# Decays between the tokens of a chunk: differences of running sums in place of masked products summed by TensorE

## The chip, the cores and the metric

The kernel runs on one core of one Trainium2 chip. The metric is the device time of one execution in microseconds, taken as the median of several executions. TensorE is called PE in the profile (PEld its weight loads), VectorE DVE, ScalarE ACT, GpSimd POOL, and SP is the queue that issues the transfers.

## The reference, cut to what matters

The reference is a two-layer backbone for 256 context tokens and 256 latent tokens of width 1,024. Each layer mixes the tokens with three parallel head groups (an S5 scan, a gated delta rule with 4 heads, a Mamba-2 block with 16 heads), each in both directions, and then applies a feed-forward block (dense in layer 0, eight experts in layer 1). What the change touches are the decays between tokens of one chunk. With `cs` the running sum of a head's log decays along the chunk, the reference forms

```python
def seg_decay(cs):
    """cs (..., T) cumulative log-decays -> (..., T, T) with [i, j] = exp(cs_i - cs_j) for i >= j, else 0."""
    diff = cs[..., :, None] - cs[..., None, :]
    return jnp.where(mask, jnp.exp(jnp.where(mask, diff, 0.0)), 0.0)
```

and multiplies it into the products of queries and keys. All log decays are negative or zero, so a decay is at most 1. The second direction reads the tokens backwards.

## The kernel before, in words

Everything is laid out for 512 tokens (context and latent together) as four token tiles of 128. The method `mixer` builds one layer's token mixing: it normalises the tokens into `hH` and `hL`, projects them with `proj` (weights are streamed by `wload`, which copies each into a rounded half `wH` on ACT, line 321, and a remainder `wL` on DVE, line 322, and `mm3` multiplies the three products of halves), convolves (`conv_silu`, four multiply-adds `cv_acc` on DVE at line 800), runs the S5 scan (`s5B`, `s5t`, lines 609 and 612 on DVE), the delta rule (`gdn_prep`, `gdn` with its triangular inverses `iv_X`, `iv_Q`) and Mamba-2 (`m2`).

The order of the instructions on every engine is fixed when the program is built. A planner places instructions by the priority of the band in which they are written (`self.band(...)`, numbers out of the table `Q`; a lower number is more urgent) and by its own estimate of when their inputs are there. Each engine then works through its list in order, and an instruction at the head that still waits holds up all behind it.

`smalls` computes, for each token, the 40 log decays `la` (two directions of 16 Mamba-2 heads and 4 delta-rule heads). It splits them into a rounded half and a remainder, `la2` (lines 742 to 746), and sums them along the tokens with six small matmuls per layer (lines 755 to 761).

`decay_quad` (lines 769 to 781) makes the decays of 4 heads and one token tile, both directions multiplied together: a tile of 128 by 4 times 128. For each direction GpSimd writes a tile `dq_r` (line 776): 8 columns of `la2` (4 heads, both halves), each spread over 128 columns and masked by an affine select. TensorE multiplies it twice (halves) by a triangular matrix `tri_r`, all four products into one bank of PSUM, and ACT takes the exponential out of the bank (line 781). There are 32 such calls: in each layer 4 in `gdn_prep` (line 856, one per token tile, result `gd_W`, banks `px`, one buffer for `dq_r`), and in `m2_decays` (lines 1060 to 1067, result `dq_W`, written to the scratch `WD` by a transfer, banks `bg`, two buffers for `dq_r`) 16 in layer 0 and 8 in layer 1, where only the two latent tiles need them. This is 64 affine selects and 128 matmuls in all. The banks `bg` are three in layer 0 (5, 6, 7) and two in layer 1 (6, 7); `px` has two (2, 3) while `gdn_prep` runs. `m2` loads the decays back from `WD` (line 1158), some time later.

Of the kernel before, what the change touches and what calls it, by code (L numbers as in the profile page):

```python
# [10 lines left out]
F32 = mybir.dt.float32  # L11
F32R = mybir.dt.float32r
# [38 lines left out]
NC16 = 50  # L51


def _cst():
# [7 lines left out]
    out += [c16 == r % 16, c16 > r % 16, c16 < r % 16, (r // 16) % 2 == np.arange(2)[None, :]]  # L62
    return np.concatenate([np.asarray(m, np.float32) for m in out], axis=1)
# [27 lines left out]
class Net:  # L91
    def __init__(self, ctx, tc, A, out, dump=None):
# [10 lines left out]
        cst = c.tile([128, ncst * 128 + NC16], F32, name="cst")  # L103
# [17 lines left out]
        self.tri_r = c.tile([128, 2, 128], F32R, name="tri_r")  # L121
        nc.vector.tensor_copy(self.tri_r[:, 0, :], self.gt)
        nc.vector.tensor_copy(self.tri_r[:, 1, :], self.lt)
# [585 lines left out]
    def smalls(self, l, p, tp, h):  # L709
# [44 lines left out]
        lav = la.rearrange("p t (d h) -> p d t h", d=2)  # L754
        for d in range(2):
# [11 lines left out]
        return dict(sp=sp, dde=dde, la=la2.bitcast(F32), beta=beta, cs=ex[:, 0], de=ex[:, 1], tot=ex[:, 2])  # L767

    def decay_quad(self, p, sm, t, h0, out, tag, bufs):

        nc = self.nc
        ps = self.ps(tag)
        for d in range(2):
            r = p.tile([128, 8, 128], F32R, name="dq_r", bufs=bufs)
            v = sm["la"][:, t, d * 5 + h0 // 4].rearrange("p x h -> p (x h)")
            nc.gpsimd.affine_select(r, v.unsqueeze(2).to_broadcast([128, 8, 128]), pattern=[[0, 8], [1 if d == 0 else -1, 128]],
                                    compare_op=OP.is_ge, fill=0.0, base=0, channel_multiplier=-1 if d == 0 else 1)
            for x in range(2):
                self.mm(ps, self.tri_r[:, d, :], r[:, x * 4:x * 4 + 4].rearrange("p h c -> p (h c)"), start=(d + x == 0),
                        stop=(d + x == 2))  # L780
        nc.scalar.activation(out, ps.rearrange("p (h c) -> p h c", h=4), AF.Exp)
# [1214 lines left out]
```

## Time and profile before

| quantity | value |
|---|---|
| time, median of 3 executions | 2483.29 us (2481.88 to 2485.01) |
| time of the profiled execution | 2479.87 us |
| span of the profiled execution | 2478.1 us |
| busy share of the span: PE, DVE, ACT, POOL | 93%, 75%, 57%, 10% |
| mean granted clock of TensorE | 0.974 of full |

The span is the stretch between the first and the last instruction of one profiled execution; its time is 1.8 us longer, and the median of the timed executions is 3.4 us above that. The shares are means over stages that are limited by different engines, so a stage has to be read by itself. Layer 0's mixer lies at about 60 to 600 us, layer 1's at about 1,120 to 1,600 us, and the experts fill the rest.

### The profile page before, as it was taken

Reading aid. Unit: us, or ns where it says so; the run is one execution under the profiler, and the core shown is the slowest. Engines: PE = TensorE matmul, PEld = TensorE weight load, DVE = VectorE, ACT = ScalarE, POOL = GpSimd, SP = SyncE. Lnnn points to the kernel's source line nnn. Section 1 sums busy time; section 2 is a strip of 40 time slices with the busy share of each in tenths; the row PEclk is TensorE's granted clock in tenths of the full one; section 3 lists DMA queues with packets and bytes.
Section 4 is the critical chain, followed back from the end, with each engine's and each line's share of the span. In section 5 each row is a group of like instructions: output and inputs, shape, how many; then the busy total and the mean of one; then the engine's idle time right before and its main releaser. Section 6 shows DMA issues by size and latency. Waiting matters only on the chain.

```text
span 2478.1 us, 36217 instructions
## 1 busy us (share of the span) xinstructions
PE 2296.1 (93%) x12886; PEld 1843.6 (74%) x12886; DVE 1868.1 (75%) x3138; ACT 1419.7 (57%) x2200; POOL 257.3 (10%) x332
## 2 busy tenths in 40 slices
PE   7999887898999999998998799889999999999998
PEld 4878675666767777886887677778887888888876
DVE  8887995576577773436679867678888888888887
ACT  4765475343335343235764844357777777677765
POOL 0011553212000000000021522100000000000000
PEclk9999998997999999998999899989999999999999
DMA  7443336994455755323444474478999999999994
GB/s 254 134 125 121 112 122 215 268 277 146 122 204 176 255 179 185 94 89 101 149 135 130 157 209 123 133 290 316 332 335 362 349 338 337 356 342 341 354 344 167
DMA packets 222378, 543.86 MB, mean 219 GB/s; under 512 B 25584, under 2 KB 105456, under 8 KB 186096
## 3 DMA queue, kind: packets, MB, share of 16 engines
q1 hardware_dynamic: 222192, 541.49, 63.7%
q8 instruction: 103, 1.69, 0.3%
q14 instruction: 83, 0.68, 0.1%
HBM read 487.87 MB, written 53.54 MB: 218 GB/s over the span
## 4 chain that ended last, share of the span: by engine, by line
PE 65%; DVE 6%; DMA 5%; ACT 4%; issue 3%; POOL 0%; SPq 0%; ACTq 0%; DVEq 0%; POOLq 0%
PE bank L162 62%; DMA ada<-in_ada_w_dram 1%; ACT mwH L1673 1%; DVE mwL L1674 1%; DVE wL L322 1%; PE bank L1761 1%; DMA wr<-in_w_in_dram 1%; DVE s5B L612 0%; DMA s5X<-XD 0%; DVE s5t L609 0%; DVE cv_acc L800 0%; DMA vD<-gd_tok 0%; PE bank L933 0%; DMA s5V<-VD 0%; DMA yr<-yD 0%
## 5 line engine op out<-in xcount | busy, mean ns | idle before, releaser
L1674 DVE TENSOR_TENSOR mwL<-mwr,mwH 128x2048 fp32r<-128x2048 f32 (+1 forms) x272 | 605.1, 2226 | 96.5 <-PE bank L162 60.3
L1673 ACT ACTIVATE mwH<-mwr 128x2048 fp32r<-128x2048 f32 (+1 forms) x272 | 508.2, 1869 | 201.6 <-PE bank L162 168.8
L321 ACT ACTIVATE wH<-wr 128x512 fp32r<-128x512 f32 (+2 forms) x388 | 232.8, 605 | 389.6 <-PE bank L162 241.2
L322 DVE TENSOR_TENSOR wL<-wr,wH 128x512 fp32r<-128x512 f32 (+2 forms) x388 | 267.0, 690 | 209.5 <-ACT wH L321 204.7
L162 PE MATMUL bank<-mwL,xeH 128*128 128x512 f32 (+1 forms) x768 | 292.7, 381 | 9.3 <-DVE mwL L1674 9.3
L162 PE MATMUL bank<-mwH,xeL 128*128 128x512 f32 (+1 forms) x768 | 288.1, 375 | 0.0
L162 PE MATMUL bank<-mwH,xeH 128*128 128x512 f32 (+1 forms) x768 | 284.7, 376 | 2.5 <-ACT mwH L1673 2.5
L162 PE MATMUL bank<-hH,wH 128*128 128x512 f32 (+2 forms) x656 | 245.8, 383 | 32.0 <-ACT cv_acc L798 18.6
L162 PE MATMUL bank<-hH,wL 128*128 128x512 f32 (+2 forms) x656 | 245.6, 376 | 8.7 <-DVE wL L322 8.5
L162 PE MATMUL bank<-hL,wH 128*128 128x512 f32 (+2 forms) x656 | 246.6, 376 | 1.1 <-DVE hL L300 1.1
L162 PEld LDWEIGHTS bank<-mwL,xeH 128*128 128x128 f32 x768 | 144.3, 188 | 37.7 <-DVE mwL L1674 11.7
L162 PEld LDWEIGHTS bank<-hH,wH 128*128 128x128 f32 (+1 forms) x656 | 124.0, 190 | 61.7 <-ACT cv_acc L798 20.7
L162 PEld LDWEIGHTS bank<-mwH,xeH 128*128 128x128 f32 x768 | 144.1, 188 | 32.3 <-ACT mwH L1673 3.3
L162 PEld LDWEIGHTS bank<-mwH,xeL 128*128 128x128 f32 x768 | 144.3, 188 | 26.3
L800 DVE SCALAR_TENSOR_TENSOR cv_acc<-cv_raw,pp,cv_acc 128x512 f32<-128x512 f32 (+1 forms) x192 | 152.8, 811 | 7.5 <-ACT cv_acc L796 5.8
L162 PEld LDWEIGHTS bank<-hH,wL 128*128 128x128 f32 (+1 forms) x656 | 124.4, 190 | 33.7 <-DVE wL L322 10.7
L162 PE MATMUL bank<-yo,wH 128*128 128x512 f32 (+1 forms) x512 | 133.2, 351 | 11.5 <-ACT yo L1387 7.7
L162 PEld LDWEIGHTS bank<-hL,wH 128*128 128x128 f32 (+1 forms) x656 | 124.7, 190 | 25.3 <-DVE hL L300 2.9
L162 PE MATMUL bank<-fhH,wH 128*128 128x512 f32 x352 | 137.6, 394 | 2.7 <-ACT fhH L299 1.8
L162 PE MATMUL bank<-mwL,eaH 128*128 128x512 f32 x352 | 139.2, 395 | 0.0
L162 PE MATMUL bank<-mwH,eaL 128*128 128x512 f32 x352 | 138.6, 394 | 0.0
L162 PE MATMUL bank<-fhL,wH 128*128 128x512 f32 x352 | 137.9, 392 | 0.0
(449 smaller groups left out, 4531.2 us busy)
## 6 DMA issues: line engine op xcount, KB each, us to landing
mwr<-in_moe_gu_dram SPq DMA_DIRECT2D x176, 1024.0 KB, 5.7
mwr<-in_moe_dn_dram SPq DMA_DIRECT2D x80, 1024.0 KB, 6.0
wr<-in_w_in_dram SPq DMA_DIRECT2D x160, 256.0 KB, 2.9
ada<-in_ada_w_dram SPq DMA_DIRECT2D x24, 1024.0 KB, 7.1
wr<-in_w_out_dram SPq DMA_DIRECT2D x64, 256.0 KB, 2.7
ada<-in_ada_w_dram SPq DMA_DIRECT2D x32, 512.0 KB, 6.0
wr<-in_ffn_w_gate_dram SPq DMA_DIRECT2D x44, 256.0 KB, 2.7
wr<-in_ffn_w_up_dram SPq DMA_DIRECT2D x44, 256.0 KB, 2.8
```

Source lines behind the costliest of these rows:

```text
L162: return self.nc.tensor.matmul(*a, **k)
L321: nc.scalar.activation(wH, w, AF.Copy)
L322: nc.vector.tensor_tensor(wL, w, wH.bitcast(F32), op=OP.subtract)
L800: nc.vector.scalar_tensor_tensor(acc, raw[:, :, j:j + 256], w[:, j:j + 1], acc, op0=OP.mult, op1=OP.add)
L1673: nc.scalar.activation(wH, w, AF.Copy)
L1674: nc.vector.tensor_tensor(wL, w, wH.bitcast(F32), op=OP.subtract)
L1761: nc.tensor.transpose(pt[:, j * 128:(j + 1) * 128], a[:, j * 128:(j + 1) * 128], self.ident)
```

## The change

The masked products are gone. `smalls` now puts the log decays of all heads and tiles side by side (`lc`, twice), and four matmuls per layer with a matrix `mid` give, for every head and tile, one row of 128 running sums, measured from the middle of the tile. A copy on ACT rounds them, and a subtraction on DVE puts the remainder into the lower half of the same tile; the rows of the Mamba-2 heads (128 partitions: 64 rounded, 64 remainders) and of the delta-rule heads (64 partitions) are kept as `rows`. `decay_heads`, called once before the loops of `gdn_prep` and of `m2_decays`, spreads the rows over 4 head columns with a mask, one multiplication per direction. `decay_quad` then forms the difference of running sums of each direction in a bank of its own, with two matmuls (a column of a selection matrix, repeated 128 times, against the spread rows; the rows against a negative selection, repeated along 128 columns). ACT copies the first bank out, DVE takes the minimum with the second bank (for every pair of tokens one of the two directions is the masked one, with a difference of at least zero), and ACT takes the exponential from SBUF to SBUF.

```diff
-        self.tri_r = c.tile([128, 2, 128], F32R, name="tri_r")
-        nc.vector.tensor_copy(self.tri_r[:, 0, :], self.gt)
-        nc.vector.tensor_copy(self.tri_r[:, 1, :], self.lt)
+        self.sel = c.tile([128, NSEL], F32R, name="sel")
+        nc.vector.tensor_copy(self.sel, cst[:, ncst * 128 + NC16:])
+        self.mid = c.tile([128, 2, 128], F32, name="mid")
+        for d, m in enumerate((self.le, self.ge)):
+            nc.vector.tensor_scalar(self.mid[:, d], m, m[:, 63 + d:64 + d], None, op0=OP.subtract)
...
-        la2 = p.tile([128, 4, 10, 2, 4], F32R, name="la2")
-        laH, laL = [la2[:, :, :, i, :].rearrange("p t q h -> p (t q) h") for i in range(2)]
-        la4 = la.rearrange("p t (q h) -> p (t q) h", h=4)
-        nc.vector.tensor_copy(laH, la4)
-        nc.vector.tensor_tensor(laL, la4, laH.bitcast(F32), op=OP.subtract)
...
+        lc = tl("sm_lc", [128, 2, 192])
+        nc.vector.memset(lc[:, :, 128:192], 0.0)
+        for x in range(2):
+            nc.vector.tensor_copy(lc[:, :, 64 * x:64 * x + 64].rearrange("p d (t h) -> p d t h", t=4), lav[:, :, :, 0:16])
+            nc.vector.tensor_copy(lc[:, :, 128 + 32 * x:144 + 32 * x].rearrange("p d (t h) -> p d t h", t=4),
+                                  lav[:, :, :, 16:20])
+        pr = self.ps()
+        for d in range(2):
+            for x in range(2):
+                nr = 64 if x else 128
+                self.mm(pr[0:nr, (2 * x + d) * 128:(2 * x + d + 1) * 128], lc[:, d, 128 * x:128 * x + nr],
+                        self.mid[:, d], start=True, stop=True, skip_group_check=True)
+        rows = []
+        for x, nr in ((0, 128), (1, 64)):
+            r = p.tile([nr, 2, 128], F32R, name=f"rows{x}")
+            v = pr[0:nr, 256 * x:256 * x + 256].rearrange("p (d c) -> p d c", d=2)
+            nc.scalar.activation(r, v, AF.Copy)
+            nc.vector.tensor_tensor(r[nr // 2:], v[nr // 2:], r[nr // 2:].bitcast(F32), op=OP.subtract)
+            rows.append(r)
...
-    def decay_quad(self, p, sm, t, h0, out, tag, bufs):
-
-        nc = self.nc
-        ps = self.ps(tag)
+    def decay_heads(self, p, sm, x):
+
+        r = sm["rows"][x]
+        m = p.tile([r.shape[0], 2, 4, 128], F32R, name="dq_r")
         for d in range(2):
-            r = p.tile([128, 8, 128], F32R, name="dq_r", bufs=bufs)
-            v = sm["la"][:, t, d * 5 + h0 // 4].rearrange("p x h -> p (x h)")
-            nc.gpsimd.affine_select(r, v.unsqueeze(2).to_broadcast([128, 8, 128]), pattern=[[0, 8], [1 if d == 0 else -1, 128]],
-                                    compare_op=OP.is_ge, fill=0.0, base=0, channel_multiplier=-1 if d == 0 else 1)
-            for x in range(2):
-                self.mm(ps, self.tri_r[:, d, :], r[:, x * 4:x * 4 + 4].rearrange("p h c -> p (h c)"), start=(d + x == 0),
-                        stop=(d + x == 2))
-        nc.scalar.activation(out, ps.rearrange("p (h c) -> p h c", h=4), AF.Exp)
+            self.nc.vector.tensor_tensor(m[:, d], r[:, d].bitcast(F32).unsqueeze(1).to_broadcast([r.shape[0], 4, 128]),
+                                         self.sel[0:r.shape[0], 0:4].bitcast(F32).unsqueeze(2).to_broadcast([r.shape[0], 4, 128]),
+                                         op=OP.mult)
+        return m
+
+    def decay_quad(self, sm, m, x, g, out, tag):
+
+
+        nc = self.nc
+        r = sm["rows"][x]
+        n = r.shape[0]
+        quad, own = (self.sel[0:n, 84:88], self.sel[0:n, 88:104]) if x else (self.sel[:, 4:20], self.sel[:, 20:84])
+        ps = [self.ps(tag) for d in range(2)]
+        for d in range(2):
+            self.mm(ps[d], quad[:, g:g + 1].to_broadcast([n, 128]), m[:, d].rearrange("p h c -> p (h c)"), start=True, stop=False)
+            self.mm(ps[d], r[:, d], own[:, 4 * g:4 * g + 4].unsqueeze(2).to_broadcast([n, 4, 128]), start=False, stop=True)
+        nc.scalar.activation(out, ps[0].rearrange("p (h c) -> p h c", h=4), AF.Copy)
+        nc.vector.tensor_tensor(out, ps[1].rearrange("p (h c) -> p h c", h=4), out, op=OP.min)
+        nc.scalar.activation(out, out, AF.Exp)
...
+        dm = self.decay_heads(tp, sm, 1)
         for t in range(4):
             sl = slice(t * 128, (t + 1) * 128)
             W = tp.tile(sh, F32, name="gd_W")
-            self.decay_quad(tp, sm, t, 16, W, "px", 1)
+            self.decay_quad(sm, dm, 1, t, W, "px")
...
+        dm = self.decay_heads(p, sm, 0)
         for h0 in (0, 4, 8, 12):
             for t in range(first, 4):
                 W = p.tile([128, 4, 128], F32, name="dq_W", bufs=4)
-                self.decay_quad(p, sm, t, h0, W, "bg", 2)
+                self.decay_quad(sm, dm, 0, 4 * t + h0 // 4, W, "bg")
```

The selection matrices are 104 more columns of the constant `cst`, whose second transfer is issued at 15.4 us and grows by 53 KB.

## Rows read from the trace of the kernel before

**Rows 1.** Busy time of each engine over the whole span, from the page.

```profile
PE 2296.1 (93%) x12886; PEld 1843.6 (74%) x12886; DVE 1868.1 (75%) x3138; ACT 1419.7 (57%) x2200; POOL 257.3 (10%) x332
```

**Rows 2.** By window: PE, PEld, DVE, ACT, POOL, clock, DMA share, GB/s.

```profile
176.00:222.00 46.00, 45.02 (x302) 38.20 (x301) 30.21 (x66) 29.18 (x57) 13.70 (x7) 1.00 0.47 139
...
267.00:398.00 131.00, 103.87 (x570) 81.43 (x569) 130.44 (x188) 74.26 (x130) 73.01 (x70) 0.95 0.36 117
398.00:420.00 22.00, 15.00 (x128) 11.40 (x127) 6.28 (x10) 21.73 (x38) 1.28 (x1) 0.92 0.75 243
...
1394.00:1428.00 34.00, 28.02 (x185) 23.20 (x183) 33.72 (x41) 29.06 (x52) 21.62 (x26) 1.00 0.62 197
```

**Rows 3.** VectorE by form, 267 to 398 us: busy us, mean ns, idle.

```profile
L800 DVE SCALAR_TENSOR_TENSOR cv_acc<-cv_raw,pp,cv_acc 128x512 f32<-128x512 f32 x46 | 43.2, 948 | 0.0
L612 DVE TENSOR_TENSOR s5B<-s5B,s5t 128x512 f32<-128x512 f32 x22 | 21.7, 992 | 0.0
L322 DVE TENSOR_TENSOR wL<-wr,wH 128x512 fp32r<-128x512 f32 x22 | 21.3, 968 | 0.0
L609 DVE TENSOR_TENSOR s5t<-s5B,s5l 128x512 f32<-128x512 f32 x22 | 18.1, 847 | 0.0
L609 DVE TENSOR_TENSOR s5t<-s5B,s5l 128x448 f32<-128x448 f32 x6 | 5.6, 960 | 0.0
L940 DVE TENSOR_TENSOR iv_Q<-bank,cst 128x512 f32<-128x512 f32 x8 | 5.4, 678 | 0.0
...
L612 DVE TENSOR_TENSOR s5B<-s5B,s5t 128x448 f32<-128x448 f32 x6 | 5.2, 861 | 0.0
```

**Rows 4.** Timeline of VectorE, 378 to 392 us; start us, duration us.

```profile
379.61 0.74 DVE L800 SCALAR_TENSOR_TENSOR cv_acc<-cv_raw,pp,cv_acc 128x512 f32<-128x512 f32 x1
...
380.88 0.68 DVE L612 TENSOR_TENSOR s5B<-s5B,s5t 128x512 f32<-128x512 f32 x1
...
382.08 1.57 DVE L800 SCALAR_TENSOR_TENSOR cv_acc<-cv_raw,pp,cv_acc 128x512 f32<-128x512 f32 x1
383.58 1.57 DVE L612 TENSOR_TENSOR s5B<-s5B,s5t 128x512 f32<-128x512 f32 x1
...
386.57 0.68 DVE L940 TENSOR_TENSOR iv_Q<-bank,cst 128x512 f32<-128x512 f32 x1
```

**Rows 5.** Timeline of GpSimd, 378 to 392 us.

```profile
380.04 10.48 POOL L776 TENSOR_SCALAR_AFFINE_SELECT dq_r<-la 128x1024 fp32r<-128x1024 f32 x6 [6.37 <-PE bank L162]
```

**Rows 6.** Groups of GpSimd instructions by form, 267 to 398 us.

```profile
L776 POOL TENSOR_SCALAR_AFFINE_SELECT dq_r<-la 128x1024 fp32r<-128x1024 f32 x32 | 53.4, 1691 | 9.3 <-PE bank L162 8.7 <-DVE gd_x L892 0.3 <-POOL cv_raw L791 0.3
```

**Rows 7.** Instructions on the tile dq_r; ns minimum, median, maximum.

```profile
L162 PE MATMUL bank<-dq_r,tri_r x128: 387/397/797, 175.5 to 1434.7; 128*128 128x512 f32 x128
L776 POOL TENSOR_SCALAR_AFFINE_SELECT dq_r<-la x64: 1093/1538/6542, 90.7 to 1430.6; 128x1024 fp32r<-128x1024 f32 x64
```

**Rows 8.** Instructions on the tile dq_W; ns minimum, median, maximum.

```profile
L781 ACT ACTIVATE dq_W<-bank x24: 597/598/640, 293.3 to 1435.2; 128x512 f32<-128x512 f32 x24
```

**Rows 9.** Groups of GpSimd instructions by form, 1,394 to 1,428 us.

```profile
L776 POOL TENSOR_SCALAR_AFFINE_SELECT dq_r<-la 128x1024 fp32r<-128x1024 f32 x15 | 20.4, 1375 | 4.5 <-PE bank L162 4.5
```

**Rows 10.** Groups of VectorE instructions by form, 1,394 to 1,428 us.

```profile
L800 DVE SCALAR_TENSOR_TENSOR cv_acc<-cv_raw,pp,cv_acc 128x512 f32<-128x512 f32 x15 | 15.2, 1025 | 0.3 <-ACT cv_acc L798 0.2
L322 DVE TENSOR_TENSOR wL<-wr,wH 128x512 fp32r<-128x512 f32 x7 | 7.1, 1020 | 0.0
```

**Rows 11.** What TensorE waited for, 176 to 222 us.

```profile
PE bank L162 <- POOL dq_r L776: 1.0, 1, 1.0
```

**Rows 12.** TensorE waits, 267 to 398 us: total us, times, longest.

```profile
PE bank L162 <- POOL dq_r L776: 6.9, 9, 1.6
```

**Rows 13.** Timeline of TensorE around 1,200 us.

```profile
1199.71 1.46 PE L162 MATMUL bank<-sm_la,cst 128*128 128x80 f32 x12
```

**Rows 14.** By window, the first 60 us, columns as before.

```profile
0.00:60.00 60.00, 43.05 (x358) 24.96 (x359) 52.70 (x241) 24.73 (x52) 0.85 (x7) 1.00 0.75 262
```

**Rows 15.** Groups of ScalarE instructions, whole span: table loads at the exponential.

```profile
L781 ACT ACT_TABLE_LOAD x23 | 29.5, 1283 | 5.6 <-issue 3.2 <-PE bank L162 2.1
```

More of the change, by code (lines that the diff above doesn't have):

```diff
@@ L51 @@
 NC16 = 50
+NSEL = 104
 def _cst():
@@ L62, in _cst @@
     out += [c16 == r % 16, c16 > r % 16, c16 < r % 16, (r // 16) % 2 == np.arange(2)[None, :]]
+    r4, r16 = r % 64, r % 32
+    out += [r % 4 == np.arange(4)[None, :], r4 // 4 == c16, -1.0 * (r4 == np.arange(64)[None, :]),
+            (r16 // 4 == np.arange(4)[None, :]) & (r < 64), -1.0 * ((r16 == c16) & (r < 64))]
     return np.concatenate([np.asarray(m, np.float32) for m in out], axis=1)
@@ L102, in __init__ @@
         ncst = len(CST) + 2 * len(LEVELS)
-        cst = c.tile([128, ncst * 128 + NC16], F32, name="cst")
+        cst = c.tile([128, ncst * 128 + NC16 + NSEL], F32, name="cst")
         self.bands, self.ma, self.cur = {}, {}, None
@@ L766, in smalls @@
                                 sp.rearrange("p t (d h) -> p d t h", d=2)[:, :, :, 0:16], op=OP.mult)
-        return dict(sp=sp, dde=dde, la=la2.bitcast(F32), beta=beta, cs=ex[:, 0], de=ex[:, 1], tot=ex[:, 2])
-    def decay_quad(self, p, sm, t, h0, out, tag, bufs):
+        return dict(sp=sp, dde=dde, rows=rows, beta=beta, cs=ex[:, 0], de=ex[:, 1], tot=ex[:, 2])
+    def decay_heads(self, p, sm, x):
[7 more added lines that the diff above has]
+    def decay_quad(self, sm, m, x, g, out, tag):
         nc = self.nc
-        ps = self.ps(tag)
+        r = sm["rows"][x]
+        n = r.shape[0]
+        quad, own = (self.sel[0:n, 84:88], self.sel[0:n, 88:104]) if x else (self.sel[:, 4:20], self.sel[:, 20:84])
+        ps = [self.ps(tag) for d in range(2)]
         for d in range(2):
-            r = p.tile([128, 8, 128], F32R, name="dq_r", bufs=bufs)
-            v = sm["la"][:, t, d * 5 + h0 // 4].rearrange("p x h -> p (x h)")
-            nc.gpsimd.affine_select(r, v.unsqueeze(2).to_broadcast([128, 8, 128]), pattern=[[0, 8], [1 if d == 0 else -1, 128]],
-                                    compare_op=OP.is_ge, fill=0.0, base=0, channel_multiplier=-1 if d == 0 else 1)
-            for x in range(2):
-                self.mm(ps, self.tri_r[:, d, :], r[:, x * 4:x * 4 + 4].rearrange("p h c -> p (h c)"), start=(d + x == 0),
-                        stop=(d + x == 2))
-        nc.scalar.activation(out, ps.rearrange("p (h c) -> p h c", h=4), AF.Exp)
+            self.mm(ps[d], quad[:, g:g + 1].to_broadcast([n, 128]), m[:, d].rearrange("p h c -> p (h c)"), start=True, stop=False)
[3 more added lines that the diff above has]
+        nc.scalar.activation(out, out, AF.Exp)
     def conv_silu(self, p, ps, w, b, out):
```

## The prediction, made before the change was run

> **What bounds the kernel now.** I read the busy shares first [rows 1]: PE is busy 93% of the span, DVE 75%, POOL 10%. By these means the change would do nothing, since it leaves PE's four matmuls per quad and moves work from POOL to DVE and ACT. So I asked where the tile `dq_r` is made and cut the busy time at those places [rows 2]. Three stretches hold nearly all of it. From 176 to 222 us (`gdn_prep` of layer 0) PE works 45.0 of 46 us. From 267 to 398 us (`m2_decays` of layer 0 beside the S5 scan and the convolutions) it is DVE that is full, 130.4 of 131 us, with PE at 103.9 and ACT at 74.3; when it ends, ACT alone is full to 420 us, copying out the finished scan. From 1,394 to 1,428 us (layer 1) DVE works 33.7 of 34 us and ACT 29.1. So the long stretch, 131 us, is DVE's, and a microsecond of DVE there is a microsecond of the kernel as long as no other engine fills up.
>
> The groups by form show why DVE is full there [rows 3]: instructions that take 0.68 to 0.74 us elsewhere have means of 0.85 to 0.99 us, and only `iv_Q`, which reads one operand out of PSUM, keeps 0.68. The timeline shows it one by one [rows 4]: a `cv_acc` takes 0.74 us and an `s5B` 0.68 at 380 us, and 1.57 us each from 382 us on, while POOL works through six affine selects without a pause [rows 5]; `iv_Q` between them takes 0.68. So an affine select stretches DVE instructions that read both operands from SBUF, by up to 0.89 us.
>
> **The change, part by part.**
>
> *The affine selects go.* In the 131 us stretch 32 of them hold POOL for 53.4 us [rows 6]. What they cost DVE: the excess over 0.74 us of 46 `cv_acc` is 9.2 us, over 0.68 of 22 `s5B` 6.7, of 22 `wL` 6.3, of 22 `s5t` 3.1, and over some 0.61 (0.68 less the narrower width) of the twelve instructions of 448 columns 3.5, together 28.8 us [rows 3, 4]. Other work of POOL can stretch them too: the affine selects are 53.4 of POOL's 73.0 us there, 73% [rows 2, 6]. By that share they cost 21 us, the lower end. The upper end is one full stretch for each, 32 times 0.89, 28.5 us, which is nearly all of the excess. I take 23, or 0.72 us for each select, nearer the share, because the rest of POOL's work there is long instructions as well.
>
> The Trainium skill, SBUF — State Buffer, section "Who interferes with whom", says that a DVE instruction with two SBUF inputs contends with a GpSimd instruction that reads SBUF, and that the second to start is blocked for the whole of the first. By that, each select could cost its own undisturbed length, at the shortest 1.09 us [rows 7], so 34.9 us and not 23. The trace agrees on which instructions are stretched, but shows at most 0.89 us for one.
>
> *The minimum comes.* One per quad on DVE, 512 columns, one operand from PSUM. The nearest row is `iv_Q`, also PSUM with SBUF, 0.68 us long; in a full list such instructions start 0.60 apart (two from 380.88 to 382.08, the second not shown) [rows 3, 4]. 16 quads cost 9.6 us, and the two multiplications of `decay_heads` 1.2 us more, both inputs in SBUF. Together 10.8 us; at 0.68 each, 12.2. So DVE needs 130.4 − 23 + 10.8 = 118.2 us in this stretch, **12.2 us less** (17.7 less at the upper end, 21 against 12.2 at the lower, 8.8 less).
>
> *Two ACT instructions for one.* The exponential took 0.60 us out of PSUM [rows 8]; the copy is another of that form, the exponential from SBUF I take at the same. 16 more are 9.6 us: ACT goes from 74.3 to 83.9 us, PE stays at 103.9, and DVE at 118.2 remains the fullest [rows 2]. So I let the whole 12.2 us through. The cover is thin: PE has 14 us left. The stretch from 398 us on, where ACT is full, must not receive these copies; it starts when the scan ends, with DVE.
>
> *Layer 1, 1,394 to 1,428 us.* 15 selects (20.4 us of POOL) [rows 9]; the two widest forms show 4.1 us of stretch in `cv_acc` and 2.3 in `wL` [rows 10], and at 0.72 each it would be 10.8. Eight minima and two multiplications add 6.0. DVE would gain 0.4 to 4.8 us, but ACT, at 29.1 of 34 us [rows 2], gets eight copies, 4.8 us, and is full at 33.9. I put this stretch at **0**, between −4.8 and +4.8, where the copies come on top.
>
> *`gdn_prep`.* A quad now has copy and minimum ahead of the exponential, 0.60 + 0.68 us, and no select ahead of its matmuls; PE waited 1.0 us for one in the 46 us that it bounds [rows 11]. Take **−1.0 us**. The two `px` banks are both taken by one quad, so the products of a tile must be out before the next; DVE has 16 us free there [rows 2], which covers 8 minima over both layers. In the DVE-bound stretch PE waited 6.9 us for selects [rows 12]; that idleness lies inside DVE's time and is not counted again.
>
> *PE.* Four matmuls of 512 columns before and after, so no change if repeated columns are read at the usual pace, 0.40 us for one [rows 7]. The trace has no such matmul; were half of the 64 in layer 0's long stretch to take twice that, 12.8 us more, PE's 14 us of room there would just hold them. I take 0. New are four matmuls of 128 columns per layer. Twelve of 80 columns of the same operand types took 1.46 us [rows 13], so four take about 0.8 by width, 1.6 us in both layers, and the PE is full there: **+1.6 us**. The small copies, subtractions and masks of `smalls` replace two on DVE; eight instructions narrower than 512 columns are under 4.8 us per layer, beside a PE-bound stretch where DVE works 30.2 of 46 us [rows 2]: 0. At the start DVE works 25.0 of 60 us [rows 14]; the cast of `sel`, which waits for the second transfer of `cst`, and the 53 KB hide there.
>
> *Waits added.* A quad's matmuls now wait for the minimum of an earlier quad to free the bank; behind them stands PE's whole list, the projections first. The minimum waits for the copy, and behind it stands DVE's list. The transfer to `WD` waits longer, and behind it on SP stand the weights.
>
> Sum: −12.2 + 0 − 1.0 + 1.6 = −11.6 us on the profiled execution's own 2479.9 us, so 2468.3. The median of the runs is 3.4 us above that execution, hence **2472 us**, 0.5% faster. A measurement tells about 0.2%, 5 us, from no change.
>
> **The rivals.**
>
> *The minimum stalls DVE (slower).* ACT loaded tables 23 times ahead of the 32 exponentials, 1.28 us each [rows 15]. If the copy sits behind such a load in ACT's list, a DVE that never idles now waits 1.28 us per quad: 16 times 1.28 = 20.5 us against 12.2 gained, +8.3 in layer 0; in layer 1 eight, 10.2 against at most 2.6 by its middle, +7.6; with −1.0 and +1.6 it gives 2500 us. It decides from 12.2 / 16 = 0.76 us per quad. For it: the order is fixed by a plan, and DVE is late against it already. Against: the load is needed for the exponential, which comes after the minimum.
>
> *The gain is taken up by another limit (no change).* If PE, with 14 us of room and waits on DVE's results in between, lets a quarter through, −3 − 1.0 + 1.6 gives 2481 us. For it: at 103.9 of 118.2 us [rows 2] PE would be 88% busy in a list whose whole order is planned anew. Against: DVE had no idle time at all although PE waits.
>
> *All of it comes out (faster still).* One full stretch per select: −17.7 − 4.8 − 1.0 + 1.6 = −21.9, 2461 us; and 2454 if PE's 6.9 us of waits for selects come free as well [rows 12].
>
> *Each select holds DVE for its whole length.* 32 times 1.09 us less 10.8 is 24.1 us in layer 0; with −4.8, −1.0 and +1.6 the time is 2455 us. Against it: no stretch above 0.89 us [rows 4]. It is what the blocking named by the Trainium skill, SBUF — State Buffer, section "Who interferes with whom", would make here.
>
> *The change doesn't take the stretch away.* If DVE is slowed by something else than the selects, 10.8 us are simply added in layer 0: 2495 us. Against it stands the timeline [rows 4, 5].
>
> **How the numbers follow.** The sum: 0.50, by itself 2464 to 2478 (8.8 to 17.7 us in place of 12.2 make 2466 to 2475, half of layer 1's ends the rest). The stall: 0.14. The gain taken up: 0.18, of which 0.04 still faster by over 0.2%. All of it: 0.11. The whole length: 0.03. The wrong cause: 0.04. So faster 0.50 + 0.04 + 0.11 + 0.03 = 0.68, the same 0.14, slower 0.14 + 0.04 = 0.18. The range runs from the fast end, 2454, to 2490, which takes in the no-change case with layer 1 at its wrong end, 2486, and stalls a little over 0.76 us, and leaves out the stall at its full price and most of the wrong cause, some 0.17.
>
> **What would show it.** Right: no `dq_r` on POOL, POOL's busy time down by the 53.4 and 20.4 us of selects in the two stretches and more; `cv_acc`, `s5B` and `wL` at 0.68 to 0.78 in the DVE-bound stretch of layer 0, which is some 12 us shorter; minima at 0.68 with no idle time on DVE before them; ACT fuller by 19 us in all. Wrong: idle time of DVE that ends with an ACT copy, PE waits that end with a minimum, matmuls on `rows` longer than 0.40 us, more table loads, or DVE's forms still at 0.95.

## The result, and the profile after

The change made the kernel slower: 2515.07 us (median of 4 executions, 2513.09 to 2520.03) against 2484.12 us on the same chip, a ratio of 1.0134 with a 95% interval of 1.0120 to 1.0147, or 31 us. The profiled execution took 2513.35 us, its span 2511.6 us (before: 2478.1), with a mean granted clock of 0.968 (0.974).

The busy line of the page, to set beside [rows 1]:

```profile
PE 2314.7 (92%) x12902; PEld 1858.2 (74%) x12902; DVE 1855.7 (74%) x3189; ACT 1433.4 (57%) x2231; POOL 158.0 (6%) x268
```

GpSimd lost 99 us of selects and DVE is 12 us lighter, as planned. TensorE is busy for 18.6 us longer, which is over half of the 33.5 us between the two spans, and it was granted 0.50, the lower of its two clock levels, for 161 us of the span in place of 131. The work meant to be relieved is the stretch in which the S5 scan of layer 0 runs. I bound it here by the scan itself, from its first `s5t` to its last. By window, columns as in [rows 2], first before, then after:

```profile
279.00:393.00 114.00, 88.38 (x423) 69.36 (x422) 114.00 (x150) 64.70 (x110) 66.47 (x60) 0.94 0.36 119
325.00:350.00 25.00, 22.20 (x114) 17.57 (x113) 25.00 (x42) 19.19 (x32) 10.42 (x14) 1.00 0.35 119
350.00:375.00 25.00, 19.54 (x105) 15.74 (x103) 25.00 (x37) 17.90 (x34) 13.98 (x13) 0.99 0.30 96
```

```profile
290.00:405.00 115.00, 93.60 (x508) 75.94 (x507) 104.80 (x176) 75.27 (x135) 14.66 (x27) 0.92 0.45 148
325.00:350.00 25.00, 22.71 (x119) 19.26 (x120) 22.13 (x37) 22.24 (x38) 0.40 (x6) 1.00 0.42 143
350.00:375.00 25.00, 25.00 (x140) 21.71 (x139) 21.82 (x47) 24.02 (x41) 0.40 (x6) 1.00 0.41 142
```

The reader is to see four things. The stretch is not shorter (115 us for 114). DVE, which never idled, now idles 10 us of it. From 325 to 375 us ACT is busy 46.3 of 50 us, where it was busy 37.1. And TensorE is busy 47.7 of these 50 us, where it was busy 41.7. The groups of DVE by form in the same stretch, before and then after (busy us, mean ns, idle us and what ended it), show that the stretch of single instructions went as forecast:

```profile
L800 DVE SCALAR_TENSOR_TENSOR cv_acc<-cv_raw,pp,cv_acc 128x512 f32<-128x512 f32 x39 | 37.2, 965 | 0.0
L612 DVE TENSOR_TENSOR s5B<-s5B,s5t 128x512 f32<-128x512 f32 x21 | 21.1, 1006 | 0.0
L322 DVE TENSOR_TENSOR wL<-wr,wH 128x512 fp32r<-128x512 f32 x19 | 18.5, 971 | 0.0
```

```profile
L834 DVE SCALAR_TENSOR_TENSOR cv_acc<-cv_raw,pp,cv_acc 128x512 f32<-128x512 f32 x38 | 28.6, 763 | 3.7 <-ACT cv_acc L832 3.7
L618 DVE TENSOR_TENSOR s5t<-s5B,s5l 128x512 f32<-128x512 f32 x22 | 17.5, 828 | 0.0
L621 DVE TENSOR_TENSOR s5B<-s5B,s5t 128x512 f32<-128x512 f32 x21 | 15.7, 752 | 0.0
L331 DVE TENSOR_TENSOR wL<-wr,wH 128x512 fp32r<-128x512 f32 x18 | 14.6, 811 | 0.0
L814 DVE TENSOR_TENSOR dq_W<-bank,dq_W 128x512 f32<-128x512 f32 x16 | 10.8, 683 | 3.2 <-ACT dq_W L813 3.2
L975 DVE TENSOR_TENSOR iv_Q<-bank,cst 128x512 f32<-128x512 f32 x10 | 6.7, 682 | 0.3 <-PE bank L171 0.3
L978 DVE TENSOR_TENSOR iv_X<-iv_X,bank 128x512 f32<-128x512 f32 x10 | 6.7, 680 | 2.9 <-PE bank L171 2.9
L797 DVE TENSOR_TENSOR dq_r<-rows,sel 128x512 fp32r<-128x512 f32 x2 | 1.3, 678 | 0.0
```

Where the 33.5 us between the two spans lie is best read by cutting the traces at the same instructions: the first and last `s5t` (the scan's), the first `fhH` (the FFN's), the first `smT` (of layer 1's `smalls`) and the last `gd_r` (of layer 1's delta rule). The table gives the length of each stage in us, with TensorE's idle time in brackets; e1, e2, e5, e10 and e14 are experiments below. Each column is one profiled execution, up to 10 us off its kernel's median (e14: 2494.5 us for 2504.0), so a few us in one stage tell little.

| stage | before | after | e1 | e2 | e5 | e10 | e14 |
|---|---|---|---|---|---|---|---|
| 60 us to the scan's first `s5t` | 219.4 (5.2) | 230.2 (6.1) | 238.8 (7.2) | 220.7 (5.2) | 226.5 (4.2) | 225.8 (6.3) | 229.4 (5.8) |
| to its last `s5t` | 112.3 (25.6) | 114.1 (21.4) | 105.7 (22.3) | 113.5 (17.5) | 113.7 (19.0) | 110.6 (25.5) | 113.8 (20.2) |
| to the FFN's first `fhH` | 332.8 (39.2) | 330.9 (48.1) | 336.8 (52.5) | 311.8 (31.0) | 329.0 (49.7) | 317.3 (28.4) | 319.9 (40.3) |
| FFN, to layer 1's `smT` | 459.0 | 464.8 | 458.5 | 460.3 | 456.9 | 463.1 | 462.1 |
| layer 1, to its last `gd_r` | 389.4 | 399.9 | 396.4 | 400.5 | 398.2 | 393.9 | 396.3 |
| to the end | 905.3 | 911.7 | 909.0 | 913.9 | 912.4 | 906.4 | 911.1 |

After against before: +10.8 us ahead of the scan, +1.8 in it, −1.9 behind it, +5.8 in the FFN, +10.5 in layer 1's mixer and +6.4 behind that. No stage gained anything to speak of, and half of the loss lies in layer 1's mixer and behind it. The 10.8 us are not all waiting or new work: TensorE runs 17 more matmuls of the projections ahead of the scan than before, some 4 us at the 0.23 us by which such matmuls follow each other.

### The profile page after: what moved, and what is told of

Its sections match the earlier page's. It is cut to its first block, busy times and chain, and to the rows that moved or that the text cites. A ratio compares the mean times of both kernels' runs of the same rounds, so it can differ in the third digit from the quotient of the medians.

```text
span 2511.6 us, 36227 instructions
## 1 busy us (share of the span) xinstructions
PE 2314.7 (92%) x12902; PEld 1858.2 (74%) x12902; DVE 1855.7 (74%) x3189; ACT 1433.4 (57%) x2231; POOL 158.0 (6%) x268
## 4 chain that ended last, share of the span: by engine, by line
PE 66%; DMA 5%; DVE 5%; ACT 4%; issue 4%; POOL 0%; SPq 0%; ACTq 0%; POOLq 0%; DVEq 0%
PE bank L171 64%; DMA ada<-in_ada_w_dram 1%; DMA s5X<-XD 1%; ACT mwH L1709 1%; DVE mwL L1710 1%; PE bank L1797 1%; DMA wr<-in_w_in_dram 1%; DMA s5V<-VD 0%; DMA s5D<-KD 0%; DMA wr<-in_ffn_w_gate_dram 0%; DVE wL L331 0%; DMA yr<-yD 0%; DVE m_E L1199 0%; ACT wH L330 0%; DMA mwr<-in_moe_gu_dram 0%
## 5 line engine op out<-in xcount | busy, mean ns | idle before, releaser
L331 DVE TENSOR_TENSOR wL<-wr,wH 128x512 fp32r<-128x512 f32 (+2 forms) x388 | 257.8, 667 | 195.9 <-ACT wH L330 187.0
L171 PE MATMUL bank<-hH,wH 128*128 128x512 f32 (+2 forms) x656 | 246.7, 384 | 35.7 <-ACT cv_acc L832 22.3
L834 DVE SCALAR_TENSOR_TENSOR cv_acc<-cv_raw,pp,cv_acc 128x512 f32<-128x512 f32 (+1 forms) x192 | 140.1, 744 | 19.1 <-ACT cv_acc L832 10.8
L171 PEld LDWEIGHTS bank<-hL,wH 128*128 128x128 f32 (+1 forms) x656 | 125.5, 191 | 25.6 <-DVE hL L309 2.9
```

What stands on the lines that cost most here:

```text
L171: return self.nc.tensor.matmul(*a, **k)
L331: nc.vector.tensor_tensor(wL, w, wH.bitcast(F32), op=OP.subtract)
L834: nc.vector.scalar_tensor_tensor(acc, raw[:, :, j:j + 256], w[:, j:j + 1], acc, op0=OP.mult, op1=OP.add)
```

## The experiments

All ratios are to the kernel before, timed on the same chip, with 95% intervals; a kernel "before" or "changed" is the one of the diff. Theories: A, the longer chain copy, minimum, exponential of `gdn_prep` costs; C, the rows' place in `smalls`; D, the new quads of `m2_decays`; B, the rival that any newly planned order costs or gains by chance. F to J came from the traces.

**e1 to e3: one part alone.** e1 makes the rows beside `la2` and uses neither rows nor the new `decay_quad`; e2 uses them in `m2_decays` only, e3 in `gdn_prep` only (each makes only its own rows). The sums run from the tile's start, with `le` and `ge` in place of `mid`.

```diff
# e1, e2, e3
-                        self.mid[:, d], start=True, stop=True, skip_group_check=True)
+                        self.ge if d else self.le, start=True, stop=True, skip_group_check=True)
...
# e1, e2: gdn_prep keeps the selects; e1, e3: m2_decays keeps them
-            self.decay_quad(sm, dm, 1, t, W, "px")
+            self.decay_old(tp, sm, t, 16, W, "px", 1)
...
-                self.decay_quad(sm, dm, 0, 4 * t + h0 // 4, W, "bg")
+                self.decay_old(p, sm, t, h0, W, "bg", 2)
```

> The kernel before, with the new rows computed in smalls beside the old tile la2 (sums from the tile's start in place of its middle, so that the constants fit) and never used: all decays still come from affine selects. Theory A (the longer chain of gdn_prep is what costs) : 2483 to 2489 us, only the small instructions. Rival B (any newly planned order costs): anywhere, 2490 to 2510, though nothing in it is heavy. Rival C (the smalls' additions hold up the first convolutions, which came 7 us late after the change): 2491 to 2500 us, first cv_acc at 97 us or later. Rival D (m2_decays' coupling of its banks to ACT and DVE): 2483 to 2489.

> New decays in m2_decays alone (16 and 8 quads); gdn_prep keeps its affine selects; of the new rows only those of the Mamba-2 heads are made, from the tile's start. Theory A: the gain predicted for the stretch appears without the loss, 2470 to 2482 us, with the 15-step loop of layer 0 starting within 3 us of before, at 236 us. Rival C: 2490 to 2500. Rival D: 2500 to 2515, the whole loss.

> New decays in gdn_prep alone (4 quads per layer); m2_decays keeps its affine selects; of the new rows only those of the delta-rule heads are made, from the tile's start. Theory A: slower by most of the loss, 2500 to 2515 us, the 15-step loop of layer 0 starting some 10 us late. Rival C: 2490 to 2500. Rival D: 2483 to 2490.

Measured: e1 1.0117 (1.0086 to 1.0148), 2514.2 us; e2 0.9993 (0.9974 to 1.0012), 2482.6 us; e3 1.0366 (1.0334 to 1.0399), 2575.4 us. So with the rows alone, which nothing reads, nearly the whole loss is there, above every range given (e1 also keeps the split into `la2`, which the changed kernel has not). The 16 and 8 new quads of `m2_decays` cost nothing, even together with the Mamba-2 heads' rows, which e2 too makes in `smalls`: D falls. In e2 the loop starts 1.4 us late, within what A asked, and the FFN starts 18 us earlier than before (706.1 us for 724.5). But layer 1 and the rest give 20 us back (table). e3 is above every range too, and not a clean test of A: its plan moved `m2_decays` behind the scan, first exponential at 505 us in place of 293, and most of its loss is there. It shows something else: the scan with no quads beside it, neither the old nor the new:

```profile
294.00:382.00 88.00, 67.48 (x375) 56.83 (x374) 85.17 (x142) 36.15 (x91) 13.21 (x20) 0.94 0.30 98
```

88 us, against 114 to 115 in the two kernels. Less of the other work stands beside it too: TensorE's records are 375, for 423 and 508.

Why do a few small instructions cost 28 us in e1? Its PE timeline (start us, duration us) shows two things at the place where they stand:

```profile
90.83 2.85 PE L171 MATMUL bank<-sm_la,cst 128*128 128x80 f32 x12
...
95.16 1.25 PE L171 MATMUL bank<-cst,sm_lc 128*128 128x128 f32 x4
96.34 2.82 PE L171 MATMUL bank<-s5U,G 128*128 128x64 f32 x12
...
99.81 1.25 PE L171 MATMUL bank<-cst,sm_lc 128*128 128x128 f32 x4
100.99 1.94 PE L171 MATMUL bank<-WV,w 128*32 128x128 f32 x32
```

The plan put other S5 work (`WV`, `s5U`) ahead of the first projection of q, k and v, as in the changed kernel, whose first `cv_acc` comes at 99.5 us for 92.4; in e1 it comes at 106.3. And the granted clock is 0.50 from 90 to 100 us (before: 1.00), so the twelve records on `la` take 2.85 us where they took 1.46 at the same place before. The second of the two is e1's own: in the changed kernel the clock is 0.97 there and the twelve take 1.56 us. And e1 starts layer 0's Mamba-2 at 445.7 us, 2.4 us late, where the changed kernel starts it 25 us late. The two kernels lose about the same, but not in the same way.

**e4 and e8: next to nothing, planned anew.** Six memsets of 64 columns, or one of 8, more in `smalls` of the kernel before.

```diff
+        for _ in range(6):                                          # e4
+            nc.vector.memset(tl("sm_nl", [128, 64]), 0.0)
+        nc.vector.memset(tl("sm_nl", [128, 8]), 0.0)                # e8
         beta = tl("beta", [128, 4, 8])
```

> The kernel before with six memsets of 64 columns more on DVE in smalls of each layer, well under 0.1 us each: next to no work, but a plan made anew. Theory A, rivals C and D: 2482 to 2488 us. Rival B (the planner's order moves by chance whatever is edited): off by more than 5 us to either side, as the changed kernel is off by 31.

> The kernel before with one memset of 8 columns more on DVE in smalls of each layer. Rival B (the planned order moves by chance with any edit): off by more than 5 us to either side. All others: within 3 us of before.

Measured: e4 1.0027 (1.0011 to 1.0044), 2491.5 us; e8 1.0009 (0.9990 to 1.0027), 2486.8 us. A memset of e4 takes 0.11 us, not under 0.1. The two plans differ: ahead of the FFN e8's DVE runs 1,268 of its 1,269 instructions in the order of before, e4's at most 1,109 of 1,278. So an order planned anew goes with some 6 us. B holds, but far below 31 us.

**e5 and e6: the rows later.** In e5, the changed kernel, the rows are made at the head of `gdn_prep` and of `m2_decays`. e6 does the same for `m2_decays` alone, with the selects in `gdn_prep`.

```diff
+        r1 = self.make_rows(tp, sm, 1, "px")     # gdn_prep, e5
         dm = self.decay_heads(...)
+        r0 = self.make_rows(p, sm, 0, "bg")      # m2_decays, e5 and e6
         dm = self.decay_heads(...)
```

> The changed kernel with its rows made where they are used, the delta rule's at the head of gdn_prep and Mamba-2's at the head of m2_decays, in place of smalls; the same work, only later and less urgent. Theory C (the rows' place ahead of the first projections costs, as the smalls alone did with +28 us): first cv_acc of layer 0 back at 92 to 94 us and the time back to 2470 to 2490 us. Theory A (gdn_prep's longer chain): still 2500 to 2515. Rival B (the planned order moves by chance): no better than before by more than the null edit showed, and the first cv_acc tells nothing of the end.

> New decays in m2_decays alone, its rows made at its head (from the tile's start); smalls and gdn_prep as before. Theory C: layer 0's gain of e2, where the FFN began 18 us earlier than before, grows by the 2 us that the first cv_acc was late, and the time is 2470 to 2482 us. Rival B: layer 0's plan falls out another way, and the FFN starts anywhere from 706 to 735 us.

Measured: e5 1.0061 (1.0039 to 1.0082), 2498.2 us, first `cv_acc` at 92.1 us; e6 1.0172 (1.0142 to 1.0202), 2524.3 us. In e5 the first convolution is back in its place and 17 us are won: the time is above C's range and below A's, so by this run the rows' place would be about half of the loss. Of the 15 us between the two profiled spans 6 are won ahead of the FFN and 8 within it. e6 is a miss of every theory: its FFN starts at 750 us, outside even the range given for B, with TensorE idle 43 us between the last `gd_r` and the FFN where e2 idles 18. The two differ only in where the rows are made, and here the move that won 17 us in e5 costs 42 (2524.3 for 2482.6). So the rows' place by itself has no fixed price; what else sets it, the planned order above all, was not taken apart.

**e7: new quads in layer 0's `m2_decays` alone.** e2, with the selects kept throughout layer 1.

```diff
+                if first == 0:
                     self.decay_quad(sm, dm, 0, 4 * t + h0 // 4, W, "bg")
+                else:
+                    self.decay_old(p, sm, t, h0, W, "bg", 2)
```

> As e2, new decays in m2_decays of layer 0 alone; layer 1 keeps the affine selects throughout. If the 12 us that e2 lost between layer 1's smalls and its end come from the new decays there, this keeps layer 0's 18 us and gives 2465 to 2473 us. Rival B (layer 1's plan falls by chance, not by what is edited): 2475 us or more, layer 1's mixer (from smT to the last gd_r) longer than before's 389 us though its instructions are those of before. Rival E (the experts' part is set by its transfers, so that an earlier start is not an earlier end): the last gd_r earlier by 15 us or more and the end earlier by less than 10.

Measured: 0.9989 (0.9973 to 1.0004), 2480.7 us. The FFN starts 14 us early (710.3 us), and layer 1, whose instructions are those of before, takes 399.4 us from `smT` to the last `gd_r` (before 389.4) and 913.0 from there to the end (905.3). So layer 1's loss is not the work of the new quads there. It is the order again (of 2,319 matmul records of layer 1's mixer 1,776 stand in the order of before), the clock, or something that the kernels with the new constants share.

**e9 to e12: one number of the plan, on both kernels.** The band of `smalls` in layer 0 from 1.0 to 1.05 (e9 changed, e10 before), or that of `m2_decays` from 1.9 to 1.5, more urgent (e11 changed, e12 before). The expectations of e11 and e12 speak of 2.1, behind the xbc convolutions (2.0); what ran is 1.5. No instruction differs.

```diff
-    pb=1.0, sc=2.5, ..., db=1.9, ..., sm=1.0, ...
+    pb=1.0, sc=2.5, ..., db=1.9, ..., sm=1.05, ...   # e9, e10
+    pb=1.0, sc=2.5, ..., db=1.5, ..., sm=1.0, ...    # e11, e12
```

> The changed kernel with one number of layer 0's priorities changed: the band of smalls 1.05 in place of 1.0, behind the projections of q, k and v. The instructions are those of the changed kernel. Theory C (the rows' place ahead of the projections): first cv_acc at 85 to 93 us and 2485 to 2500 us, as in e5. Rival B (the planned order decides, whatever the edit): off the changed kernel's 2515 by more than 5 us to either side, and its twin on the kernel before is off by more than 5 us too.

> The kernel before with the same number changed (smalls' band 1.05). Theory C: its smalls hold nothing up (first cv_acc at 92 us before), so within 5 us of 2483. Rival B: off by more than 5 us.

> The changed kernel with the band of m2_decays in layer 0 at 2.1, behind the xbc convolutions (2.0). Theory F (the freed DVE time went to convolutions, and the minima and copies fill ACT at 325 to 375 us; the S5 scan's end sets Mamba-2's start through SP's list): the xbc convolutions come even earlier, the scan ends at 410 us as before, 2510 to 2520 us. Rival B: anywhere, by more than 5 us.

> The kernel before with the band of m2_decays in layer 0 at 2.1. Theory F: the affine selects go on stretching DVE, no change above 5 us. Rival B: off by more than 5 us to either side.

Measured: e9 1.0150 (1.0104 to 1.0197); e10 0.9951 (0.9933 to 0.9969), 2475.6 us; e11 1.0110 (1.0068 to 1.0152); e12 0.9989 (0.9970 to 1.0008). In e9 the first `cv_acc` stayed late (101.7 us), so moving the band did not do what moving the rows did. e11 and e12 changed next to nothing: from 60 to 720 us TensorE runs 3,587 of 3,589 records in the order of the changed kernel, and 3,606 of 3,610 in that of before. They repeat the two kernels and test neither F nor the band of `m2_decays`. In the pair with another order (e9, e10) the times move by up to 0.5%, and the changed kernel stays the slower one. e10, the kernel before with one priority changed, is the fastest kernel measured here and faster than both.

**e13: the memory's layout.** The kernel before with 832 unused bytes per partition among the constants, which is by how much the change enlarges them.

```diff
+        pad = c.tile([128, 208], F32, name="pad")
+        nc.vector.memset(pad[:, 0:1], 0.0)
```

> The kernel before with an unused tile of 832 bytes per partition among the constants (one column of it set to zero), which is by how much the constants of the changed kernel are larger, so that every tile behind them lies elsewhere. Theory H (every kernel with the new constants lost 8 to 12 us in layer 1's mixer and 3 to 8 in the experts, also where the instructions there are those of before: it is the memory's layout): from layer 1's smT to the last gd_r 396 us or more (before: 389), from there to the end 909 us or more (before: 905), together 2492 to 2500 us. Rival B (the planned order): layer 0's mixer is off by several us to either side, layer 1 and the experts only by chance.

Measured: 1.0014 (0.9999 to 1.0030), 2487.7 us; layer 1 393.4 us, the rest 908.4. Theory H falls as the cause: some 7 of the 17 us at most, and no more than e4 lost there without it (393.3 and 908.6).

**e14, e15, e17: Mamba-2's loads on another queue.** In the changed kernel layer 0's Mamba-2 starts 25 us late (first `m_xe` at 468 us for 443), although the output of its last convolution comes 16 us earlier. SP's timeline shows the loads of `m_in` behind the scan's output and the loads that need it; first before, then after:

```profile
421.01 0.32 SPq L626 DMA_DIRECT2D XD<-s5X  x1
...
432.34 0.43 SPq L1095 DMA_DIRECT2D m_in<-mD  x1
```

```profile
431.38 3.62 SPq L635 DMA_DIRECT2D XD<-s5X  x2
...
440.81 6.70 SPq L655 DMA_DIRECT2D s5D<-KD  x7
...
451.17 0.45 SPq L1131 DMA_DIRECT2D m_in<-mD  x1
```

```diff
-                nc.sync.dma_start(i[:, 0:4], mD[:, g, 0:4, sl])
+                nc.gpsimd.dma_start(i[:, 0:4], mD[:, g, 0:4, sl])
...
```

> The changed kernel with Mamba-2's three loads of m_in issued from GpSimd's queue in place of SP's. Theory F (the scan, which ends 13 us later, holds the loads of m_in up in SP's list, so Mamba-2 starts 25 us late, and its end is not covered): the first m_xe of layer 0 at 445 us or earlier instead of 468, the FFN starting by 10 us or more earlier than 735, time 2495 to 2505 us. Rival I (m_in waits for its data or its memory and not for the queue): first m_xe at 460 us or later, time 2510 to 2520.

> The kernel before with the same three loads issued from GpSimd's queue, where the affine selects are. Theory F: Mamba-2 starts at 440 us already, little to gain, 2478 to 2488 us. Rival B: off by more than 5 us to either side.

> The two edits that won time back on the changed kernel together: rows made where they are used (e5, 17 us won) and m_in's loads on GpSimd's queue (e14, 11 us won). If they cure two separate losses they add: 2485 to 2490 us, the kernel before's time. If both work by the same link, an earlier start of Mamba-2 in layer 0 (e5's first m_xe was at 441 us already), the second adds nothing: 2496 us or more.

Measured: e14 (changed) 1.0067 (1.0047 to 1.0088), 2504.0 us, first `m_xe` at 445 us, FFN at 723.1 us; e15 (before) 1.0045 (1.0032 to 1.0058), 2495.7 us; e17 (e5 with the loads moved) 1.0115 (1.0095 to 1.0135), 2510.9 us. So e14 lies in F's ranges: the loads stand behind the late scan in SP's list, and moving them wins the changed kernel 11 us by the medians; the kernel before does not gain from the same move, it loses 10, outside F's range. The trace of e14 adds a second link. GpSimd's timeline (in brackets what the engine idled for):

```profile
433.94 0.96 POOL L1131 DMA_DIRECT2D m_in<-mD  x1 [10.61 <-DMA XD<-s5X]
```

The load itself waits for the scan's output transfers. They write another tensor, so what `m_in` needs of them is presumably the memory that they free; by that, which no run tested, the scan's end gates Mamba-2 on any queue. In e17 the second edit won nothing, it cost 13 us: its first `m_xe`, at 440 us, was at 441 in e5 already. That speaks against two losses that add up. That the one loss is the late start of Mamba-2 is not shown: e1 and e9 start it at 446 and 447 us and reach the FFN at 741 and 744 us, later than the changed kernel (735).

**e16: e7 with the band of e10.**

```diff
-    ..., sm=1.0, ...
+    ..., sm=1.05, ...
```

> The kernel of e7 (new decays in m2_decays of layer 0 alone) with the band of smalls in layer 0 at 1.05, which made the kernel before 0.5% faster. If the two gains add: FFN start at 700 us or earlier and 2468 to 2475 us. Rival B (each plan by chance): FFN start at 710 to 740 us and no faster than 2476.

Measured: 1.0028 (1.0016 to 1.0040), 2489.9 us, FFN at 724.0 us. Two edits that each brought the FFN forward by 11 to 14 us bring nothing together.

**e18: the scan first.** e14 with the band of the scan ahead of the xbc convolutions and `m2_decays`.

```diff
-    ..., sc=2.5, ...
+    ..., sc=1.5, ...
```

> The kernel of e14 with the band of the S5 scan in layer 0 at 1.5 in place of 2.5, ahead of the xbc convolutions (2.0) and of m2_decays (1.9). Theory F, as the trace of e14 mends it (m_in also waits for the memory that the scan's output transfers hold, to 434 us): DVE's freed time goes to the scan, which takes 95 to 108 us in place of 114, m_in is issued before 428 us, and the time is 2485 to 2498 us. Rival J (the scan's own chain, or the waits for ACT beside it, set its length): 112 to 116 us again, and no faster than e14 by more than 5 us.

Measured: 1.0120 (1.0099 to 1.0140), 2511.6 us; the scan takes 113.4 us from its first `s5t` to its last:

```profile
289.00:403.00 114.00, 90.79 (x490) 73.74 (x492) 104.68 (x177) 75.24 (x132) 14.67 (x27) 0.94 0.45 145
```

This is J's range. DVE has the same 9 to 10 us of idle time as in the changed kernel. J's two causes, the scan's own chain and the waits beside it, are not told apart; and the edit moved little, since 150 of DVE's 174 instructions in the scan stand in e14's order.

## Why the prediction was wrong

The measured 2515 us lie beyond the slowest of the rivals, 2500 us. Two steps of the sum failed: the 12.2 us of DVE were let through whole, and layer 0's `smalls` and layer 1 were put at nothing.

*The stretch goes away: right.* I forecast 23 us for `m2_decays` of layer 0. The six forms of [rows 3] other than `iv_Q`, counted at the instructions of after, give 38 × 0.202 (`cv_acc`) + 21 × 0.254 (`s5B`) + 18 × 0.160 (`wL`) + 22 × 0.019 (`s5t`), and 3.2 us for the ten of 448 columns, together 19.5 us (the first factor is the count after, the second the fall of the mean in us). Part of the rest may stay because GpSimd still has 14.7 us of other work beside the scan: `s5t` has a mean of 828 ns, where it had 847. The 0.89 us that I called the most for one instruction were those of the 14 us in [rows 4]; over the stretch the longest `s5B` takes 1.76 us, 1.08 above 0.68. By the rule of the Trainium skill, SBUF — State Buffer, section "Who interferes with whom", it would be 34.9 us; the measurement agrees on which instructions suffer, its longest single stretch is near the shortest select (1.09 us), and the sum of 19.5 us stays well below 34.9.

*The minimum: right.* 16 of 683 ns and two multiplications of 678 ns, 12.3 us by their lengths, the upper figure that I gave.

*"So I let the whole 12.2 us through": this step failed.* DVE's busy time in the scan fell by 9.2 us, close to the forecast, and the scan's length rose by 1.8. The freed time is idle time now, 10.1 us of it in the rows above: 3.7 before `cv_acc` and 3.2 before the minimum, both ended by ACT, and 3.2 ended by PE. I had looked at ACT's mean over the stretch, 74.3 of 131 us, and found room. The copies do not spread over the stretch; they sit between 314 and 388 us, among 16 table loads of 1.28 us, where ACT is busy 46.3 of 50 us. ACT's groups there (busy us, mean ns, idle us):

```profile
L815 ACT ACT_TABLE_LOAD x8 | 10.3, 1283 | 0.1
L835 ACT ACT_TABLE_LOAD x8 | 10.3, 1283 | 0.1
...
L815 ACT ACTIVATE dq_W<-dq_W 128x512 f32<-128x512 f32 x16 | 10.0, 630 | 3.5 <-DVE dq_W L814 3.4
L813 ACT ACTIVATE dq_W<-bank 128x512 f32<-128x512 f32 x16 | 9.3, 598 | 7.0 <-PE bank L171 5.6 <-issue 1.3
```

ACT is not the only one: TensorE, to which I had given 14 us of room, is busy 47.7 of these 50 us, and 5.6 of the 7.0 us that ACT idled before the copies ended with it. That is the rival "the gain is taken up by another limit"; two thirds of DVE's idle time ended with ACT, and what part of that was TensorE's doing is open. The rival of the table load has the right engine and the wrong price: the minimum waits for its copy 4 times, 3.2 us in all, not 16 times 1.28. Only e3 shows the stretch without any quads, 26 us shorter, and with less of the other work in it.

*"The small copies, subtractions and masks of `smalls` ... 0": this step failed.* e1, in which they are all that is new, is 28 us slower, more than twice what any harmless edit moved. I had costed them as DVE time beside a PE-bound stretch. But ahead of the scan TensorE idles 6 us in 230, and what is planned in front of the projections is in front of everything that follows: the first convolution 7 us late, the last of the S5 tables (`cm_a`) 9, the scan's start 11. In the changed kernel the delay goes on through SP's list to Mamba-2, 25 us late at its start, 14 at its last gate (`m_z`, 670 us for 656). TensorE's waits from 655 to 705 us (total us, times, longest), where a hole lies, first before, then after:

```profile
PE bank L162 <- ACT yo L1387: 3.7, 1, 3.7
```

```profile
PE bank L171 <- ACT yo L1423: 11.7, 1, 11.7
```

Of this chain e14 bears out the last part: with Mamba-2 back at 445 us TensorE does not idle at all in these 50 us, where the changed kernel idles 15.7 and the kernel before 5.0. The whole of it is argued, and other runs speak against it. e5 starts Mamba-2 at 441 us and idles 16.2 us there all the same. e10 starts its scan 6 us late and is the fastest kernel; in e16 the first convolution is 8 us late and the scan starts 1.6 us early. So that the rows are not free is seen in e1, but by which path they cost, and how much of it is the order that they bring about, is open; the opposite outcomes of e5 and e6 speak for the order, and e9, which moved the band and not the convolution, did not settle it.

*PE, +1.6 us: mis-sized.* The new matmuls of `smalls` appear as 8 records per layer, twice the four in the code, and took 1.57 us in layer 1 where I had put 0.8: I had read the twelve records of [rows 13] as twelve matmuls, and they are six. Repeated columns are read at the usual pace: the 128 matmuls of all quads take 38.2 us, each counted up to the next one's start, for 37.3 before. In all about +3.8 us.

*`gdn_prep`, −1.0 us: not borne out.* From the first `gd_kw` to the last it takes 43.6 us for 39.3, +4.3; the first quad's copy ran at 183.7 us, and its minimum came out of DVE's list only at 192.6. That both banks belong to one quad was noted and covered with "DVE has 16 us free", again a mean. But +4.3 us is not the price of the longer chain: e5 has the same new quads there and takes 38.7 us, and e10 has the selects and takes 45.6. The order moves this stage by more than the kind of quad, and what the chain costs is not settled.

*Layer 1, 0 ± 4.8 us: wrong in size, and not for the reason given.* It lost 10.5 us, and lost 10.0 in e7 with the instructions of before. One part can be read from the clock. e4, e8, e10 and e13 run layer 1's mixer on all four engines in exactly the order of before, and still take 387.6 to 393.9 us; the time goes with how long TensorE was granted 0.50 in it:

| layer 1's mixer | before | e8 | e4 | e13 | e10 | e7 | changed |
|---|---|---|---|---|---|---|---|
| length, us | 389.4 | 387.6 | 393.3 | 393.4 | 393.9 | 399.4 | 399.9 |
| at 0.50 of the clock, us | 20.5 | 20.5 | 23.9 | 30.7 | 30.7 | 30.7 | 37.5 |

At 0.50 a matmul takes twice as long (2.85 us for 1.46, above), so the 17 us more of it in the changed kernel explain at most half as much, 8.5 of the 10.5 us; over the whole span it is 30 us more, at most 15 of the 33.5 us. Why the clock was lower there, and whether that is the order's doing, no run shows. Behind layer 1's mixer the time at 0.50 did not grow (28 us for 32), and TensorE's matmuls stand in the order of before; for these 6.4 us no cause is shown. Against the kernel before, its other versions differ in layer 1's mixer and the experts together by −1 to +9 us (e8, e4, e15), every kernel with new decays by +11 or more; the memory's layout is not it (e13).

*Is it only a bad draw of the planner?* By these runs, hardly. Six other versions of the kernel before, none with new work to speak of (e4, e8, e10, e12, e13, e15), lie at 0.9951 to 1.0045; the changed kernel and its six variants (e5, e9, e11, e14, e17, e18) at 1.0061 to 1.0150. The medians do not overlap, though the intervals of e15 and e5 do, and e8, e11 and e12 are hardly new draws. e1, the kernel before with the unused rows, lies with the second (1.0117). On this, a draw is worth up to ±0.5% and the change with its rows about +1%. New decays in `m2_decays` alone lie among the first in three versions of four (e2, e7, e16; e6 does not). The bound that I gave this measurement, 0.2%, lies within the intervals of the runs here (±0.12 to ±0.47%) and is too small for two plans.

## What to carry to other kernels

Where a planner fixes the order, an edit is costed by where it stands as well as by what it holds, and even then not by its own length: the same rows in `smalls` came with 28 us in e1 and, those of the Mamba-2 heads beside the new quads, with nothing in e2. Room is read in the part of the stretch where the new instructions will sit; a mean over 131 us said 57% for ACT, which was then 93% busy for 50 of them, with TensorE at 95%. And before a gain of half a per cent is ascribed to an edit, some harmless edits planned anew show how much the order alone moves, and stages that kept their order show how much the clock does.

## What was not expected of the hardware

In e1 TensorE was granted 0.50 of its clock, the lower of its two levels, from 90 to 100 us while it was busy 10.0 of 10 us. By window, columns as in [rows 2], first before, then the changed kernel, then e1:

```profile
80.00:90.00 10.00, 8.43 (x64) 6.95 (x62) 5.84 (x21) 7.01 (x21) 0.25 (x4) 0.83 0.22 70
90.00:100.00 10.00, 10.00 (x66) 8.25 (x65) 7.85 (x12) 9.29 (x17) 1.37 (x5) 1.00 0.31 123
```

```profile
80.00:90.00 10.00, 7.80 (x52) 6.26 (x51) 7.85 (x23) 7.57 (x23) 0.32 (x4) 0.69 0.30 99
90.00:100.00 10.00, 9.65 (x122) 8.69 (x121) 1.54 (x7) 6.02 (x14) 0.00 (x0) 0.97 0.26 107
```

```profile
80.00:90.00 10.00, 7.82 (x50) 6.37 (x48) 8.23 (x25) 7.16 (x23) 0.32 (x4) 0.69 0.30 94
90.00:100.00 10.00, 10.00 (x47) 9.11 (x46) 0.29 (x1) 2.62 (x6) 0.00 (x0) 0.50 0.26 105
```

From 70 to 90 us TensorE had idled 2.9 us in e1 and 1.6 before. But it idled 2.9 us in the changed kernel too, at the same 0.69 from 80 to 90 us, and there the clock was back. So the idle time alone does not tell the two apart, and what does is not shown. Ahead of the scan e1 was at 0.50 for 20.5 us, the kernel before for 3.4 and the changed kernel for 6.8: the difference to before is worth at most 8.5 of e1's 28 us. That stretches so much alike get such different clocks was not expected.
